# A list scheduler that books the SBUF port of VectorE and GpSimd, with instruction times from a trace

## The chip, the cores and the metric

The program runs on one core of one Trainium2 chip. The metric is device time in microseconds; the time before is the median of 3 runs, 1514.28 us (1511.14 to 1516.61).

## What is computed

A decoder trunk of two layers over one sequence of 512 tokens with 1024 channels, all in float32. Each layer scales and shifts its input by a projection of a condition vector (adaLN), multiplies by one input matrix, and mixes tokens in three ways: a gated recurrence (HGRN2, 256 columns), sparse attention with compressed, selected and windowed keys (512 columns), and a gated MLP over chunks (256 columns). The three are joined by an output matrix, and a squared-ReLU MLP follows. Cut to what matters here:

```python
for l in range(DEPTH):                                   # 2
    sh1, sc1, g1, sh2, sc2, g2 = split(silu(c) @ w_ada[l] + b_ada[l])
    proj = (x * (1 + sc1) + sh1) @ w_in[l]               # 1024 -> 2840
    mix = concat([hgrn2(...), nsa(...), gmlp(...)]) @ w_o[l]
    x = layer_norm(DN_ALPHA * x + (1 + g1) * mix, ln1_w[l], ln1_b[l])
    h = x * (1 + sc2) + sh2
    y = square(relu(h @ w_ff1[l])) @ w_ff2[l]            # 1024 -> 4096 -> 1024
    x = layer_norm(DN_ALPHA * x + (1 + g2) * y, ln2_w[l], ln2_b[l])
```

## The kernel before, in words

**Arithmetic.** A float32 product is made of three float32r products: every operand is split into a high part (a rounding copy, CAST or ACTIVATE) and a low part (a subtraction), and TensorE does high x high, high x low and low x high (`mm3`). Weights are split as they arrive (`wunit`: tiles `whi` and `wlo` of 128x512 or 128x256). The layer's input is transposed on TensorE and scaled, shifted and split into eight pairs `hT` (`make_hT`, two halves of 256 tokens, eight tiles each: an affine copy out of PSUM, a cast for the high part, a subtraction for the low part).

**Stages, once per layer.** Scaled input `hT`; the projections hq, hf and nq; the gated recurrence (tiles `hx` and `hbd`, seven levels); the projections of keys and values and the compressed keys; eight attention units with the remaining projections as filler between them; the state of the recurrence; the output projection (`w_o`) with the first LayerNorm; `make_hT` again, inside `ff`; the MLP in four groups; the second LayerNorm. `affine_rows` (line 1623 before) writes the normalised rows times weight plus bias to the residual stream in DRAM: 16 products and 16 sums of 128x512 tiles `xs`, all on GpSimd, in the stretch in which `make_hT` runs. The adaLN projections (`ada_accs`) are products on VectorE, ScalarE or GpSimd spread over the other stages.

**What sets the order.** The code calls no engine. It writes down instructions with virtual tiles (`Plan.op`), and `Plan.schedule` (line 332 before) places all of them in a model of time: five engines, a price for each instruction (`Plan.cost`), a latency between engines, and slots of SBUF and PSUM. At each step it takes, over all engines, the instruction that can start first; on one engine it goes through the ready ones by priority, which is their place in the program plus a shift. `Plan.emit` then writes them in that order, and each engine works through its queue in that order, whatever the model thought. Some instructions have several engines to choose from: `vg` (VectorE, or GpSimd), `gv` (the other way about), `copy` (ScalarE, or VectorE), `split` (the subtraction on VectorE, or GpSimd where allowed), `scale_rows` (GpSimd, VectorE, ScalarE). The second choice opens once the instruction has been ready for 500 ns:

```python
st = max(slot_time(o, t), bank_time(o, e))
if r[2] and t < o.ready + ALT_WAIT:
    fut = min(fut, max(st, o.ready + ALT_WAIT))
    continue
if st <= t:
    ...
    cand = (t, e, o, r[2])
    break
```

So the prices decide both the order on each queue and which engine does what. In the kernel before, VectorE and GpSimd are priced as if each had SBUF to itself.

All instructions are issued at one line (563 before, 605 after), so the profile is read by tiles and shapes. Tiles of the shared SBUF class are all called `t` in the profile before; the program's names (`hT`, `xs`, `hx`, ...) are told in the text.

Of the kernel before, what the change touches and what calls it, by code (L numbers as in the profile page):

```python
# [36 lines left out]
# ---------------------------------------------------------------- planning  # L37
# Instructions are first written down with virtual tiles, then placed in time by a
# list scheduler with a rough cost of each instruction, and emitted in that order.
# [117 lines left out]
class Op:  # L157
    __slots__ = ("ahead", "alts", "prio", "seq", "reads", "writes", "succ", "nd", "ready", "vts", "newv", "eng", "end",
# [6 lines left out]
NFILL = 1  # L165
STEPS = (1, 1, 2, 2, 2)
# [22 lines left out]
class Plan:  # L189
# [17 lines left out]
    def limit(self, name, n):  # L207
        """at most n tiles of this name live at once"""
        self.add_class("#" + name, n, 0, None)
        self.lims[name] = "#" + name  # L210
# [6 lines left out]
    # ---- cost in ns  # L217
    def cost(self, eng, method, a, k):
# [4 lines left out]
        if eng == "PE":  # L223
            if method == "transpose":
                return (a[1].p1 - a[1].p0) / 1.2 + 2.5
            n = max(int(a[2].idx.size), 32)
            if a[2].dt == F32:
                return max(2 * n / 2.4, a[1].idx.size / 1.2) + 2 * n / 2.4 + 2.5
            return n / 2.4 + 2.5
# [27 lines left out]
        return 100.0  # L257

    def op(self, alts, also=()):
# [56 lines left out]
        o.nd = len(deps)  # L316
        o.succ = []
# [13 lines left out]
    # ---- placement in time  # L331
    def schedule(self):
# [7 lines left out]
               "SP": dict(PE=100.0, V=0.0, A=0.0, G=0.0, SP=0.0)}  # L340
        table = None
# [32 lines left out]
        def slot_time(o, t):  # L374
            """earliest time at which the new tiles of o can have slots; INF: not known yet"""
# [29 lines left out]

        for o in self.ops:
            if o.nd == 0:
                push(o)
# [6 lines left out]
        while n_left:  # L415
            best = None
            for e in T:
# [14 lines left out]
                for r in sorted(ready[e])[:200]:  # L432
# [3 lines left out]
                    st = max(slot_time(o, t), bank_time(o, e))  # L436
# [14 lines left out]
                if cand is None:  # L451
                    for r in pend[e]:
# [5 lines left out]
                        fut = min(fut, max(r[0] + (ALT_WAIT if r[2] else 0), slot_time(o, r[0]), bank_time(o, e)))  # L458
# [13 lines left out]
            start = t  # L472
            if e == "PE":
                load = 0.0
                if alt[1] == "matmul":
                    load = alt[2][1].idx.size / (2.4 if alt[2][1].dt == BF else 1.2)
# [30 lines left out]
            if e == "SP":  # L507
# [4 lines left out]
                dma_free = tr + nbytes / 350.0  # L512
                end = dma_free + 950
                T[e] = start + 460
            else:
                end = start + c
                T[e] = end
            o.done = True
# [25 lines left out]
    def place(self, vt):  # L544
        pool, width = self.classes[vt.cls]["pool"], self.classes[vt.cls]["width"]
        n = int(np.prod(vt.shape[1:]))
        t = pool.tile([128, width], vt.dt, name="%s_%d" % (vt.cls, vt.slot), tag="%s%d" % (vt.cls, vt.slot))
# [19 lines left out]
def trunk(ctx: ExitStack, tc: tile.TileContext, I, out, depth=L):  # L567
# [44 lines left out]
    # ------------------------------------------------------------ constants  # L612
# [12 lines left out]
    # ---- condition vector and the bias of its projection, as columns  # L625
# [21 lines left out]
    # additive masks: causal block [q, k]; compressed blocks per q tile [q, 32]  # L647
# [17 lines left out]
    # level masks of the gated recurrence: [s, t], t in the right half and s in the left half of a block  # L665
# [20 lines left out]
    # rope tables  # L686
# [33 lines left out]
    # vectors that are needed as columns: rows of 128 through the tensor engine  # L720
# [14 lines left out]
    # lower bounds  # L735
# [15 lines left out]
    # ------------------------------------------------------------ helpers  # L751
# [13 lines left out]
    def vg(method, *a):  # L765
        """a product, sum or difference of tiles in SBUF, on either engine"""
# [16 lines left out]
    def wunit(w, off, rowlen, ncols=512, nk=2, held=""):  # L783
        """two k tiles of `ncols` columns of a [*, rowlen] matrix, as high and low parts"""
# [16 lines left out]
    def k_steps(n, steps):  # L801
        """(first k, number of k) of each step over n k tiles: two at a time, or as given"""
# [5 lines left out]
    def tok_steps(xT, w, off, rowlen, ncols, kt, evac, steps=None):  # L808
        """out[tokens, cols] for four token tiles: xT k tiles (hi, lo) stationary, weights moving; a step per two k"""
# [17 lines left out]
    def col_steps(xT, w, off, rowlen, kt, evac, nc_=4, steps=None):  # L827
        """out^T[cols, tokens] for nc_ tiles of 128 columns: weights stationary, xT moving; a step per two k"""
# [945 lines left out]
    xd = x  # L1774
# [65 lines left out]
```

## Time and profile before

| what | value |
|---|---|
| runs, median of 3 (lowest to highest) | 1514.28 us (1511.14 to 1516.61) |
| profiled execution: span from first to last instruction | 1509.3 us |
| median of the runs less that span (launch and end around it, and the difference between executions) | 5.0 us |
| mean granted TensorE clock | 0.971 of full speed |
| TensorE, VectorE, ScalarE, GpSimd busy | 1376.6, 1170.3, 554.9, 462.4 us |

The profiled execution has no time of its own beside its span; sums below are made on the span and carried over to the median of the runs. PE is TensorE, PEld its weight load, DVE VectorE, ACT ScalarE, POOL GpSimd. An instruction counts as busy from when the engine takes it, so time that it waits for something that has no semaphore is inside its duration.

### The profile page before, as it was taken

To read this page: it belongs to the slowest core of one execution; us is meant where nothing else is said; L and a number is where in the kernel's file an instruction comes from. 1 tells how busy PE (TensorE), PEld (TensorE's weight loads), DVE (VectorE), ACT (ScalarE), POOL (GpSimd) and SP (SyncE) were. 2 spreads that over 40 slices of the span, in tenths; PEclk is the share of its full clock that TensorE was granted. 3 is DMA by queue.
4 is the path that set the end of the run, shared out by engine and by line. 5 is a ranking of instruction groups with operands and counts; after the bars stand their busy time and mean duration, and the time that the engine had idled before them with its cause. 6 is when DMAs were issued, how large, how long until landed. Compare 5 with 4: busy or idle time off the path is not lost.

```text
span 1509.3 us, 21620 instructions
## 1 busy us (share of the span) xinstructions
PE 1376.6 (91%) x7459; PEld 1151.8 (76%) x7459; DVE 1170.3 (78%) x2477; ACT 554.9 (37%) x1465; POOL 462.4 (31%) x601
## 2 busy tenths in 40 slices
PE   6867888999879999999998789999896999999996
PEld 4756777777768887888887769888785888888885
DVE  9999979999978557486789995999996663444658
ACT  6541567783203313122314344877421311101121
POOL 6676577453420001010036642223424000000003
PEclk9888999999989999999999899999999999999998
DMA  9521454225466325275414115111454331233331
GB/s 314 183 72 51 119 179 136 71 83 180 152 221 211 132 88 181 97 255 175 147 42 136 35 49 148 30 57 52 147 173 153 126 103 55 94 99 98 111 112 56
DMA packets 119845, 185.69 MB, mean 123 GB/s; under 512 B 9796, under 2 KB 47160, under 8 KB 119736
## 3 DMA queue, kind: packets, MB, share of 16 engines
q1 hardware_dynamic: 119736, 184.31, 38.1%
q8 instruction: 59, 0.97, 0.3%
q14 instruction: 50, 0.41, 0.1%
HBM read 175.89 MB, written 8.39 MB: 122 GB/s over the span
## 4 chain that ended last, share of the span: by engine, by line
PE 64%; DVE 25%; issue 4%; ACT 4%; POOL 2%; DMA 2%; SPq 0%; POOLq 0%; DVEq 0%; ACTq 0%
PE ps L563 64%; DVE t L563 21%; ACT t L563 3%; DVE amax L563 1%; POOL t L563 1%; DMA t<-in_w_ada_dram 1%; DMA raw<-in_w_ada_dram 1%; POOL lnmv L563 1%; DVE acoef L563 1%; DMA t<-in_ln_w_dram 0%; DVE hst L563 0%; POOL hms L563 0%; DVE lt L563 0%; DVE adat L563 0%; POOL gmv L563 0%
## 5 line engine op out<-in xcount | busy, mean ns | idle before, releaser
L563 PE MATMUL ps<-t,t 128*128 128x512 f32 (+5 forms) x6096 | 1261.7, 363 | 72.3 <-DVE t L563 67.2
L563 PEld LDWEIGHTS ps<-t,t 128*128 128x128 f32 x6096 | 1016.5, 193 | 251.8 <-DVE t L563 40.7
L563 ACT ACTIVATE t<-ps 128x512 f32<-128x512 f32 (+11 forms) x462 | 179.0, 413 | 539.9 <-PE ps L563 528.0
L563 POOL TENSOR_TENSOR t<-t,t 128x512 f32<-128x512 f32 (+5 forms) x244 | 241.4, 1004 | 255.4 <-ACT t L563 133.1
L563 DVE TENSOR_TENSOR t<-raw,t 128x512 fp32r<-128x512 f32 (+2 forms) x376 | 248.2, 678 | 13.7 <-ACT t L563 7.2
L563 POOL TENSOR_TENSOR t<-raw,t 128x512 fp32r<-128x512 f32 (+2 forms) x56 | 65.6, 1176 | 535.7 <-ACT t L563 368.5
L563 DVE TENSOR_TENSOR t<-t,t 128x512 fp32r<-128x512 f32 (+6 forms) x270 | 182.2, 694 | 5.9 <-ACT t L563 0.8
L563 DVE TENSOR_TENSOR t<-t 128x512 f32<-128x512 f32 (+1 forms) x94 | 60.1, 653 | 151.7 <-ACT t L563 151.6
L563 ACT ACTIVATE t<-raw 128x512 fp32r<-128x512 f32 (+2 forms) x241 | 128.4, 568 | 129.3 <-DMA raw<-in_w_ff_dram 107.5
L563 PE MATMUL ps<-ident,t 128*128 128x128 f32 (+1 forms) x635 | 110.7, 282 | 36.8 <-DVE t L563 20.4
L563 ACT ACTIVATE t<-t 128x512 fp32r<-128x512 f32 (+5 forms) x202 | 98.1, 510 | 112.0 <-DVE t L563 95.8
L563 PEld LDWEIGHTS ps<-ident,t 128*128 128x128 f32 (+1 forms) x635 | 75.9, 144 | 57.6 <-issue 18.3
L563 DVE TENSOR_TENSOR t<-ps,t 128x512 fp32r<-128x512 f32 (+5 forms) x237 | 109.3, 482 | 9.1 <-ACT t L563 3.9
L563 DVE SCALAR_TENSOR_TENSOR t<-raw,silc,t 128x512 f32<-128x512 f32 x98 | 74.6, 773 | 10.7 <-DMA raw<-in_w_ada_dram 9.4
L563 DVE CAST t<-raw 128x512 fp32r<-128x512 f32 (+2 forms) x191 | 81.4, 430 | 0.2
L563 ACT ACTIVATE t<-ps,amax 128x128 f32<-128x128 f32 (+3 forms) x128 | 67.3, 534 | 20.2 <-DVE amax L563 18.4
L563 DVE TENSOR_TENSOR t<-t,ps 128x512 f32<-128x512 f32 (+1 forms) x48 | 31.1, 650 | 53.7 <-PE ps L563 53.5
L563 DVE TENSOR_REDUCE amax<-ps 128x1 f32<-128x32 f32 (+4 forms) x192 | 65.5, 380 | 4.0 <-PE ps L563 3.1
L563 POOL TENSOR_SCALAR t<-t,acoef 128x384 f32<-128x384 f32 (+3 forms) x55 | 32.2, 599 | 67.6 <-DVE acoef L563 51.7
L563 ACT ACTIVATE t<-ps,adasb 128x256 f32<-128x256 f32 x48 | 23.4, 571 | 72.4 <-PE ps L563 72.4
L563 POOL TENSOR_SCALAR t<-raw,silc 128x512 f32<-128x512 f32 x48 | 37.3, 782 | 27.4 <-PE ps L563 9.9
L563 POOL TENSOR_SCALAR lnmv<-lnmv 128x1 f32<-128x1 f32 x16 | 5.6, 348 | 113.8 <-DVE lnmv L563 113.8
(141 smaller groups left out, 878.5 us busy)
## 6 DMA issues: line engine op xcount, KB each, us to landing
raw<-in_w_ff_dram SPq DMA_DIRECT2D x128, 512.0 KB, 4.5
raw<-in_w_ada_dram SPq DMA_DIRECT2D x80, 512.0 KB, 4.6
raw<-in_w_in_dram SPq DMA_DIRECT2D x49, 256.0 KB, 2.9
t<-in_w_ada_dram SPq DMA_DIRECT2D x32, 256.0 KB, 6.1
raw<-in_w_o_dram SPq DMA_DIRECT2D x16, 512.0 KB, 4.0
raw<-in_w_in_dram SPq DMA_DIRECT2D x15, 512.0 KB, 3.6
xd<-t SPq DMA_DIRECT2D x24, 256.0 KB, 2.2
t<-xd SPq DMA_DIRECT2D x24, 256.0 KB, 4.9
```

Of the source, the lines that this page charges most:

```text
L563: getattr(self.handles[e], method)(*a, **k)
```

## The change

Five things change in `Plan`. All touch only the model of time; no instruction's arithmetic is changed, and the counts stay at 7301 TensorE instructions and 470 DMAs.

1. A port is booked. `shares` says which instructions use it: all of GpSimd's but `memset` and `iota`; on VectorE those with two inputs in SBUF, and `tensor_copy` and `tensor_scalar` from SBUF to SBUF. VectorE may start one only from 69 ns before GpSimd's last one ends, GpSimd from 147 ns before VectorE's.
2. TensorE's prices: a float32r product of n columns costs n / 2.246 + 4 ns (n / 2.4 + 2.5 before), a float32 product two passes of at least 111 ns each, and a weight load 4 ns more.
3. A VectorE instruction that needs news of more than one engine starts 62 ns later for each further one.
4. A DMA moves 310 bytes per ns (350 before).
5. Tiles are named by the program's names in the profile.

```diff
+OPEN_V, OPEN_G = 69.0, 147.0
+WAIT = 62.0
...
             if a[2].dt == F32:
-                return max(2 * n / 2.4, a[1].idx.size / 1.2) + 2 * n / 2.4 + 2.5
-            return n / 2.4 + 2.5
+                return 2 * max(2 * n / 2.4 + 2.5, 111.0)
+            if a[2].dt == BF:
+                return n / 2.4 + 2.5
+            return n / 2.246 + 4.0
...
+    def shares(self, eng, method, a, k):
+
+        if eng == "G":
+            return method not in ("memset", "iota")
+        if eng != "V" or method == "memset":
+            return False
+        out = k.get("out", a[0] if a else None)
+        ins = [x for x in list(a[1:]) + [x for n, x in k.items() if n != "out"] if isinstance(x, VA)]
+        ins = [v for v in ins if v.vt.cls not in self.psum and (v.idx.size > 1 or out.idx.size == 1)]
+        if method in ("tensor_copy", "tensor_scalar"):
+            return bool(ins) and out.vt.cls not in self.psum
+        return len(ins) > 1
...
+        def port_time(o, ai, e):
+            if e not in port or not o.port[ai]:
+                return 0.0
+            return port["G"] - OPEN_V if e == "V" else port["V"] - OPEN_G
...
-                    st = max(slot_time(o, t), bank_time(o, e))
+                    st = max(slot_time(o, t), bank_time(o, e), port_time(o, r[2], e))
...
+            if e == "V" and news > 1:
+                start += WAIT * (news - 1)
...
-                    load = alt[2][1].idx.size / (2.4 if alt[2][1].dt == BF else 1.2)
+                    load = 4 + alt[2][1].idx.size / (2.4 if alt[2][1].dt == BF else 1.2)
...
-                dma_free = tr + nbytes / 350.0
+                dma_free = tr + nbytes / 310.0
...
+                if e in port and o.port[ai]:
+                    port[e] = end
```

**What moves.** Over the whole program VectorE goes from 2477 to 2250 instructions, GpSimd from 601 to 753, ScalarE from 1261 to 1336 (table loads and accumulator reads left out). By the part of the program that an instruction belongs to:

| part | VectorE | GpSimd |
|---|---|---|
| layer 0 up to the attention (and the setup) | 438 to 402 | 187 to 218 |
| layer 0 attention | 363 to 324 | 117 to 146 |
| layer 0 `make_hT` in `ff` | 40 to 31 | 20 to 25 |
| layer 0 MLP | 423 to 392 | 38 to 48 |
| layer 1 up to the attention | 299 to 252 | 78 to 112 |
| layer 1 attention | 366 to 338 | 77 to 94 |
| layer 1 MLP | 369 to 351 | 19 to 34 |

First place: VectorE in layer 1, second half of the tokens of `make_hT` inside `ff`, before. The rows follow the last normalised row tile; a CAST makes a high part, a TENSOR_TENSOR of 128x256 a low part.

```order
L563 TENSOR_SCALAR t_32_12619<-t_32_12619,lnmv_12648 128x512
L563 CAST t_54_12509<-t_40_12700 128x256
L563 SCALAR_TENSOR_TENSOR t_44_12569<-ps_12690,t_44_12569 128x512
L563 TENSOR_TENSOR t_59_12519<-t_40_12700,t_54_12509 128x256
L563 CAST t_68_12514<-t_63_12707 128x256
L563 CAST t_12_12528<-t_36_12714 128x256
L563 TENSOR_TENSOR t_43_12522<-t_63_12707,t_68_12514 128x256
L563 TENSOR_TENSOR t_34_12536<-t_36_12714,t_12_12528 128x256
L563 CAST t_65_12545<-t_60_12731 128x256
L563 CAST t_22_12547<-t_62_12741 128x256
L563 TENSOR_TENSOR t_58_12541<-t_57_12722,t_9_12533 128x256
```

Five more such rows and one weight subtraction follow, before VectorE goes on with the weights. The same place after, VectorE:

```order
L605 TENSOR_SCALAR r_12619<-r_12619,lnmv_12636 128x512
L605 TENSOR_SCALAR hf_66_12709<-ps_12693,adasb_7551 128x256
L605 CAST hT_12532<-hf_0_12705 128x256
L605 SCALAR_TENSOR_TENSOR grow_12560<-ps_12707,grow_12560 128x512
L605 TENSOR_SCALAR hf_30_12734<-ps_12716,adasb_7551 128x256
L605 TENSOR_TENSOR hT_12527<-hf_12_12697,hT_12516 128x256
L605 TENSOR_TENSOR hT_12545<-hf_66_12709,hT_12535 128x256
L605 TENSOR_TENSOR hT_12562<-hf_30_12734,hT_12554 128x256
L605 TENSOR_TENSOR wlo_12775<-wraw_12215,whi_12761 128x512
```

and GpSimd, where before only the `xs` of `affine_rows` stood:

```order
L605 TENSOR_TENSOR xs_12700<-r_12315,lnw_12568 128x512
L605 TENSOR_TENSOR xs_12721<-r_12320,lnw_12568 128x512
L605 TENSOR_TENSOR hT_12521<-hf_60_12688,hT_12511 128x256
L605 TENSOR_TENSOR hT_12540<-hf_0_12705,hT_12532 128x256
L605 TENSOR_TENSOR hT_12557<-hf_75_12727,hT_12549 128x256
L605 TENSOR_TENSOR hT_12573<-hf_59_12738,hT_12564 128x256
L605 TENSOR_TENSOR hT_12581<-hf_77_12743,hT_12571 128x256
L605 TENSOR_TENSOR xs_12700<-xs_12700,lnb_12578 128x512
```

Of the sixteen casts and subtractions of this half VectorE did fourteen; it keeps one cast and three subtractions; five subtractions stand on GpSimd ahead of the rest of `xs`, and seven casts on ScalarE. VectorE does two affine copies out of PSUM in their stead.

Second place: the start of the gated recurrence in layer 0 (tiles `hx`, `hbd`). GpSimd after, where one `hx` or `hbd` follows the other:

```order
L605 TENSOR_TENSOR hx_1261<-hgk_973,hgq_938 128x512
L605 TENSOR_TENSOR hx_1272<-hgk_985,hgq_944 128x512
L605 TENSOR_TENSOR hx_1287<-hb_1277 128x8x32
L605 TENSOR_TENSOR hx_1290<-hb_1277 128x16x16
L605 TENSOR_TENSOR hx_1294<-hb_1277 128x32x8
L605 TENSOR_TENSOR hx_1290<-hb_1277 128x16x16
L605 TENSOR_TENSOR hbd_817<-hx_1287,hgq_938 64x4x64 x2
L605 TENSOR_TENSOR hx_1294<-hb_1277 128x32x8
```

and VectorE after, in the same stretch of the plan, in which the rotary products of the query projections (out of PSUM, tiles `acc`) now stand between the levels instead of behind them:

```order
L605 TENSOR_TENSOR hx_1355<-hb_1277 128x256
L605 TENSOR_TENSOR hx_1352<-hb_1309 128x128x2
L605 TENSOR_TENSOR hx_1357<-hb_1309 128x256
L605 TENSOR_SCALAR sin_81<-sin_81 128x4x32
L605 TENSOR_TENSOR ropet_1369<-acc_355,sin_81 128x4x32
L605 TENSOR_TENSOR ropet_1371<-acc_355,sin_81 128x4x32
L605 TENSOR_TENSOR ropet_1375<-acc_398,sin_81 128x4x32
```

There are 16 such products of 128x4x32 and 8 of 128x256 in a row. The query projection of the second half, which came after the recurrence before, is moved ahead of most of its levels.

## Rows read from the trace of the kernel before

**Rows 1.** The page, part 1: span, busy time and share of two engines

```profile
span 1509.3 us, 21620 instructions
PE 1376.6 (91%) x7459; PEld 1151.8 (76%) x7459; DVE 1170.3 (78%) x2477; ACT 554.9 (37%) x1465; POOL 462.4 (31%) x601
```

**Rows 2.** By stretch, us busy: PE, PEld, DVE, ACT, POOL, granted clock, DMA share, GB/s

```profile
0.00:198.00 198.00, 150.61 (x903) 129.79 (x903) 178.42 (x445) 90.04 (x226) 124.58 (x203) 0.91 0.51 158
198.00:339.00 141.00, 128.30 (x894) 107.41 (x894) 135.72 (x358) 108.12 (x368) 88.39 (x109) 0.99 0.33 100
...
397.00:426.00 29.00, 15.86 (x119) 14.42 (x118) 26.32 (x30) 5.27 (x12) 25.08 (x22) 0.91 0.26 82
426.00:778.00 352.00, 351.09 (x1557) 286.27 (x1558) 241.66 (x413) 83.77 (x149) 21.74 (x17) 0.99 0.49 163
778.00:936.00 158.00, 133.19 (x910) 120.85 (x909) 133.15 (x299) 60.45 (x158) 87.61 (x108) 0.95 0.30 90
936.00:1061.00 125.00, 122.95 (x884) 104.31 (x883) 114.22 (x335) 97.94 (x342) 37.77 (x64) 1.00 0.18 57
...
1122.00:1151.00 29.00, 17.23 (x124) 15.02 (x122) 26.99 (x30) 7.40 (x15) 23.84 (x21) 0.95 0.33 117
1151.00:1490.00 339.00, 338.96 (x1481) 276.30 (x1482) 187.41 (x324) 59.15 (x103) 8.77 (x7) 0.99 0.31 97
1490.00:1509.40 19.40, 7.07 (x54) 6.61 (x53) 14.26 (x25) 2.78 (x5) 9.66 (x11) 0.74 0.30 109
```

**Rows 3.** What PE waited for, five stretches in order: us in total, times, longest

```profile
PE ps L563 <- DVE t L563: 29.0, 16, 8.6
...
PE ps L563 <- DVE t L563: 9.7, 14, 2.2
...
PE ps L563 <- DVE t L563: 13.0, 4, 8.5
...
PE ps L563 <- DVE t L563: 21.7, 15, 5.6
...
PE ps L563 <- DVE t L563: 11.8, 4, 6.6
```

**Rows 4.** Timeline of DVE from 395 us, first half of make_hT: start, us, count

```profile
395.04 0.49 DVE L563 CAST t<-t 128x256 fp32r<-128x256 f32 x2
395.44 0.76 DVE L563 TENSOR_TENSOR t<-t,t 128x256 fp32r<-128x256 f32 x2
```

**Rows 5.** DVE by shape, 409 to 426 us, second half: count, busy us, mean ns

```profile
L563 DVE TENSOR_TENSOR t<-t,t 128x256 fp32r<-128x256 f32 x8 | 9.4, 1202 | 0.0
L563 DVE CAST t<-t 128x256 fp32r<-128x256 f32 x7 | 8.2, 1209 | 0.0
```

**Rows 6.** Timeline of POOL from 405 us: the products and sums of affine_rows

```profile
405.47 19.37 POOL L563 TENSOR_TENSOR t<-t,t 128x512 f32<-128x512 f32 x14
```

**Rows 7.** DVE by shape, 198 to 339 us: source in PSUM and in SBUF

```profile
L563 DVE TENSOR_TENSOR t<-ps,t 128x512 fp32r<-128x512 f32 x40 | 25.9, 681 | 0.6 <-PE ps L563 0.2 <-ACT t L563 0.2
...
L563 DVE TENSOR_TENSOR t<-raw,t 128x512 fp32r<-128x512 f32 x4 | 4.9, 1216 | 0.0
```

**Rows 8.** DVE by shape, 500 to 540 us, inside the MLP

```profile
L563 DVE TENSOR_TENSOR t<-raw,t 128x512 fp32r<-128x512 f32 x14 | 9.0, 685 | 0.1
```

**Rows 9.** DVE and POOL by shape, whole span

```profile
L563 DVE SCALAR_TENSOR_TENSOR t<-t,t 128x256 f32<-128x256 f32 x16 | 6.4, 416 | 0.1
...
L563 DVE TENSOR_TENSOR t<-ps,sin 128x128 f32<-128x128 f32 x32 | 8.8, 286 | 0.3
...
L563 POOL TENSOR_TENSOR t<-t,t 128x256 f32<-128x256 f32 x49 | 40.6, 833 | 44.7 <-DVE t L563 33.2 <-ACT t L563 10.5
```

**Rows 10.** DVE by shape, 778 to 936 us, where make_hT of layer 1 runs

```profile
L563 DVE TENSOR_TENSOR t<-t,t 128x256 fp32r<-128x256 f32 x10 | 9.1, 942 | 0.0
L563 DVE CAST t<-t 128x256 fp32r<-128x256 f32 x8 | 9.0, 1154 | 0.0
```

**Rows 11.** The chain that ended last, piece from 1135 us: start, us, engine, count

```profile
1135.39 15.61 DVE t L563 x13
```

More of the change, by code (lines that the diff above doesn't have):

```diff
@@ L157 @@
 class Op:
-    __slots__ = ("ahead", "alts", "prio", "seq", "reads", "writes", "succ", "nd", "ready", "vts", "newv", "eng", "end",
+    __slots__ = ("ahead", "alts", "port", "deps", "eng_no", "prio", "seq", "reads", "writes", "succ", "nd", "ready", "vts", "newv", "eng", "end",
                  "tabs", "banks", "done")
@@ L316, in op @@
         o.nd = len(deps)
+        o.deps = list(deps)
         o.succ = []
@@ L340, in schedule @@
                "SP": dict(PE=100.0, V=0.0, A=0.0, G=0.0, SP=0.0)}
+        count = {e: 0 for e in T}
+        seen = {e: {} for e in T}
         table = None
@@ L404, in bank_time @@
             return max([vt.bank_end for vt in o.banks if vt.bank_eng != e], default=0.0)
+        def port_time(o, ai, e):
+            if e not in port or not o.port[ai]:
+                return 0.0
+            return port["G"] - OPEN_V if e == "V" else port["V"] - OPEN_G
         for o in self.ops:
+            o.port = [self.shares(*alt) for alt in o.alts]
             if o.nd == 0:
@@ L457, in schedule @@
                             continue
-                        fut = min(fut, max(r[0] + (ALT_WAIT if r[2] else 0), slot_time(o, r[0]), bank_time(o, e)))
+                        fut = min(fut, max(r[0] + (ALT_WAIT if r[2] else 0), slot_time(o, r[0]), bank_time(o, e),
+                                           port_time(o, r[2], e)))
                     if fut < INF:
@@ L472, in schedule @@
             start = t
+            o.eng_no = (e, count[e])
+            count[e] += 1
+            news = 0
+            last = {}
+            for d in o.deps:
+                x, i = d.eng_no
+                last[x] = max(last.get(x, -1), i)
+            for x, i in last.items():
+                if i > seen[e].get(x, -1):
+                    seen[e][x] = i
+                    news += 1
+            if e == "V" and news > 1:
+                start += WAIT * (news - 1)
             if e == "PE":
@@ L546, in place @@
         n = int(np.prod(vt.shape[1:]))
-        t = pool.tile([128, width], vt.dt, name="%s_%d" % (vt.cls, vt.slot), tag="%s%d" % (vt.cls, vt.slot))
+        t = pool.tile([128, width], vt.dt, name="%s_%d" % (vt.name, vt.slot), tag="%s%d" % (vt.cls, vt.slot))
         ap = t[:vt.shape[0], :n]
```

## Prediction
> **What bounds the kernel now.** The page comes first: TensorE is busy 1376.6 of 1509.3 us [rows 1], so 132.7 us at most are to be had without making its work shorter. Then the stretches between the changes of stage [rows 2]. The two MLPs, 426 to 778 us and 1151 to 1490 us, are TensorE's: it is busy 351.1 of 352 us and 339.0 of 339, and nothing that the other engines do better there can show. The attention of layer 1 is nearly so (123.0 of 125). Time without TensorE work lies elsewhere: 47.4 us in the opening (198 less 150.6), 12.7 in the attention of layer 0, 13.1 at the first LayerNorm (397 to 426), 24.8 at the start of layer 1 (778 to 936), 11.8 at its LayerNorm (1122 to 1151) and 12.3 in the tail. These six make 122 of the 132.7.
>
> Next, the waits. In the first five of these stretches TensorE waits for VectorE 29.0, 9.7, 13.0, 21.7 and 11.8 us [rows 3]: VectorE is late, not the loads. VectorE is busy 178 of 198, 136 of 141, 26 of 29, 133 of 158 and 27 of 29 us there [rows 2].
>
> Then why VectorE is slow. In the first half of `make_hT` with GpSimd quiet, two casts of 128x256 take 0.49 us and two subtractions 0.76 [rows 4], so 245 and 380 ns each. In the second half the same shapes take 1209 and 1202 ns [rows 5], while GpSimd runs 14 products and sums of 128x512 in 19.37 us without a gap, 1384 ns each [rows 6]. Each VectorE instruction there lasts about as long as one of GpSimd's. It is not so for all: in the attention a subtraction with its source in PSUM takes 681 ns and one with both inputs in SBUF 1216 [rows 7], against 685 ns for that shape in the MLP, where GpSimd has little to do [rows 8]. So GpSimd holds VectorE up when both want SBUF, and only then. That is what the new model books.
>
> **The change, part by part.** The work is the same; what moves is who does it, and when. Instructions dropped by VectorE and taken by GpSimd stand in the table of the change; means are stretch busy time over count [rows 2].
>
> *Opening, to 198 us.* VectorE drops 36 at 401 ns (178.42/445): -14.4 us. GpSimd takes 31 at 614 ns (124.58/203): +19.0. If every one of them waits its turn at the port, the net is +4.6; if GpSimd's are all beside other work, -14.4. The order shows other work: 16 rotary products out of PSUM at 286 ns and 8 twice as wide, taken at 416 ns [rows 9], now stand beside GpSimd's run of `hx`, 7.9 us that need no port. I take 4.6 - 7.9 = **-3**.
>
> *Attention of layer 0.* VectorE drops 39 at 379 ns, -14.8; GpSimd takes 29 at 811 ns, +23.5; net +8.7 if all queue. The gain is capped by TensorE's 12.7 us of idle time. Much of VectorE's work here reads PSUM and can run beside GpSimd, which is what the model now looks for. I take about half the cap, **-6**.
>
> *First LayerNorm.* The port's queue for the second half: before, 15 casts and subtractions in 17.6 us [rows 5]. After, the order has four subtractions (4 x 0.38) and one weight subtraction (0.685) [rows 4, 8] on VectorE, three `xs` (3 x 1.38) [rows 6] and four subtractions at 833 ns [rows 9] on GpSimd: 9.7 us. That is 7.9 less. But in the new order three more `xs` stand on GpSimd ahead of the reciprocal root that the last row tile waits for: +4.2. I take **-3**; the ends are -7.9 and +4.2.
>
> *Start of layer 1.* The same `make_hT` pattern: 8 casts and 10 subtractions take 9.0 + 9.1 us [rows 10]. The order moves the 8 casts to ScalarE and 7 subtractions to GpSimd; 3 x 0.38 + 7 x 0.833 = 7.0 us, 11 less. In the whole stretch VectorE drops 47 at 445 ns (-20.9) and GpSimd takes 34 at 811 ns (+27.6), a net +6.7 where they queue. 6.7 - 11 gives -4; the port can't give more than TensorE's wait, 21.7. I take **-5**.
>
> *LayerNorm of layer 1.* Here the chain is 15.61 us of VectorE [rows 11], and nothing is put ahead of the last tile. After: one cast, three subtractions (1.4 us), two `xs` (2.8), five subtractions on GpSimd (4.2): 8.3 us. **-7**, with a cap of 11.8. ScalarE's seven casts cost nothing: it is busy 7.4 of 29 us. If it were late the casts would be late, and at most this gain goes.
>
> *Tail.* Two sums of the last row tile go from VectorE to GpSimd, the last of them on the path: 0.83 instead of 0.42 us [rows 9] and one more hand-over. **+1**; the ends are 0 and +2.
>
> *The rest.* MLPs 0: VectorE drops 31 and 18 instructions, GpSimd takes 10 and 15, all beside TensorE, which is covered by 100% busy time; without that cover GpSimd's 25 would cost some 25 us at about 1 us. The new prices of products, loads and DMA only move order, on SP too: three adaLN loads pass weight loads in the opening, with DMA engines busy 0.51 of the time. 0.
>
> Sum: -3 - 6 - 3 - 5 - 7 + 1 = -23. On the span 1509.3 that is 1486; the median of the runs lies 5.0 above, so **1491 us**.
>
> A rule against this change: the Trainium skill, GPSIMD Engine Reference, § 8 Key points, says that for elementwise work VectorE is structurally about twice as fast. The trace agrees: 833 against 416 ns for 128x256 [rows 9]. By that rule alone every instruction given to GpSimd holds the port twice as long, and opening, attention and layer 1's start would lose as in the first rival below.
>
> **The rivals.** *GpSimd's longer hold decides (slower).* The planner gives GpSimd 152 more instructions, because VectorE now looks later. In the opening, the attention and the start of layer 1 these are 94, and if all of them queue, the nets are +4.6, +8.7 and +6.7. With the LayerNorms at -3 and -7 and the tail at +1 that makes +11: **1525**. It wins from the point at which GpSimd's 94 (70 us) hold VectorE for more than the 50 us that VectorE drops there. For it: the opening keeps GpSimd 125 of 198 us busy already. Against it: TensorE waits on VectorE, not on GpSimd.
>
> *The plan doesn't hold (no change).* The queues are fixed ahead and the chip lets whoever comes first into SBUF. A plan that is off by some hundred ns puts VectorE behind GpSimd again; the stalls come back elsewhere and eat what the LayerNorms give: **1514**. For it: the model has many prices that are off by more than this.
>
> *Most stalls go (faster still).* If each of the five stretches comes half-way from my term to its end (-14.4, -12.7, -7.9, -21.7, -11.8; tail 0: -68), the sum is (-23 - 68)/2 = -46: **1468**.
>
> **How the numbers follow.** Forecast 0.55, with a range of its own of 1479 to 1504; slower rival 0.20; no change 0.13; faster still 0.12. A measurement here tells 0.3% (4.5 us) from no change. Faster is 0.55 + 0.12 = 0.67, same 0.13, slower 0.20. The range runs from 1466, just below the third rival, to 1528, just above the first; outside are the outer parts of both, some 0.15.
>
> **What would show it.** In the changed profile: busy VectorE down by more than the dropped instructions account for; casts and subtractions of 128x256 below 700 ns in the second half at both LayerNorms; TensorE's wait there below 7 us; MLP stretches unchanged within 1 us. Wrong, if GpSimd's busy time in the opening passes 145 us and VectorE's means there do not fall; if the last row tile's normalisation at the first LayerNorm comes over 4 us later than before; or if TensorE's idle total stays near 133 us.

## The result, and the profile after

The changed kernel takes **1475.37 us** (median of 4 runs, 1473.22 to 1476.26) against 1514.41 of the kernel before on the same chip (1511.14 to 1516.61): a ratio of 0.9741, 95% interval 0.9727 to 0.9756. It is faster by 39 us. The forecast was 1491, its range 1466 to 1528. The profiled spans differ by 35.7 us (1509.3 and 1473.6): the median now lies 1.8 us above the span, and lay 5.0 above it before.

The page of the changed kernel, part 1, answers to [rows 1]:

```profile
span 1473.6 us, 21673 instructions
PE 1369.8 (93%) x7459; PEld 1150.7 (78%) x7459; DVE 1104.8 (75%) x2250; ACT 588.1 (40%) x1543; POOL 589.2 (40%) x753
```

TensorE's idle time is 103.8 us (1473.6 less 1369.8), 132.7 before. Where it went is read stage by stage. A stage ends here when its last instruction ends, taken from the timeline at the same place of the program in both kernels: the last compressed value, the last low part of the attention's output, the eighth `ffa` tile of the MLP (its first group of products), and the last normalised row tile after MLP 0 or the last sum of half a row tile in MLP 1; the tail runs to the span's end. So the first LayerNorm's stage runs from the attention's end through the output projection, the normalisation and `make_hT` to the MLP's first eight tiles. The filler products have no fixed stage, so a stage can also become shorter because work left it. The last columns keep the two apart: TensorE's idle time in the stage, and its matmuls (one that crosses a border counts on both sides).

| stage, us | before | after | difference | predicted | idle before, after | matmuls before, after |
|---|---|---|---|---|---|---|
| opening of layer 0 | 203.5 | 216.4 | +12.9 | -3 | 48.6, 60.9 | 942, 969 |
| attention of layer 0 | 137.1 | 120.2 | -16.9 | -6 | 11.6, 7.1 | 861, 766 |
| first LayerNorm and `make_hT` | 122.4 | 124.1 | +1.7 | -3 | 16.2, 8.3 | 553, 623 |
| MLP 0 | 328.6 | 327.7 | -0.9 | 0 | 2.9, 1.9 | 1471, 1471 |
| start of layer 1 | 150.8 | 137.8 | -13.0 | -5 | 23.2, 11.6 | 876, 885 |
| attention of layer 1 | 117.9 | 111.3 | -6.6 | 0 | 1.7, 2.1 | 821, 769 |
| LayerNorm and `make_hT` of layer 1 | 126.8 | 116.0 | -10.8 | -7 | 16.3, 1.8 | 583, 626 |
| MLP 1 | 292.7 | 292.8 | +0.1 | 0 | 0.0, 0.0 | 1266, 1266 |
| tail | 29.5 | 27.3 | -2.2 | +1 | 12.2, 10.0 | 98, 99 |

The sum is -35.7, the difference of the spans: 28.9 us less idle time and 6.8 us less busy time. Layer 1 before its MLP gives 30.4 of it (395.5 to 365.1), 25.7 of that in idle time. Layer 0 before its MLP gives 2.3 (463.0 to 460.7) and nothing in idle time (76.4 and 76.3): the opening loses what the attention and the LayerNorm gain. Both attentions became shorter mainly because matmuls moved out of them, into the stages beside them: 95 matmuls and 12.4 us of busy time in layer 0, 52 and 7.0 us in layer 1.

**Layer 1's LayerNorm is where the change works as meant.** VectorE and then GpSimd in its second half, timelines of the changed kernel (start, us, engine):

```profile
1113.36 1.22 DVE L605 CAST hT<-hf 128x256 fp32r<-128x256 f32 x1 [0.31 <-ACT hf L605]
1114.50 0.68 DVE L605 SCALAR_TENSOR_TENSOR grow<-ps,grow 128x512 f32<-128x512 f32 x1
1115.10 0.53 DVE L605 TENSOR_SCALAR hf<-ps,adasb 128x256 f32<-128x256 f32 x1
1115.55 2.34 DVE L605 TENSOR_TENSOR hT<-hf,hT 128x256 fp32r<-128x256 f32 x3
```

```profile
1114.39 4.10 POOL L605 TENSOR_TENSOR hT<-hf,hT 128x256 fp32r<-128x256 f32 x5
1118.44 1.74 POOL L605 TENSOR_TENSOR xs<-xs,lnb 128x512 f32<-128x512 f32 x1
```

The half is done in 5.1 us (1113.36 to 1118.49), where the chain before had 15.61 us of VectorE [rows 11]. One VectorE instruction is not as fast as forecast: the cast takes 1.22 us and a subtraction 780 ns. VectorE has 4 of them here instead of 14. The chain of waits passes through this place on other engines now:

```profile
1103.58 8.01 PE acc L605 x68
1111.59 0.23 PE ps L605 x2
...
1111.85 1.49 ACT hf L605 x3
...
1115.62 2.26 DVE hT L605 x3
1117.89 1.16 DVE wlo L605
...
1119.08 2.95 PE acc L605 x15
```

TensorE is busy 13.65 of the 14 us here, 17.23 of 29 before [rows 2]. The windows (columns as in [rows 2]):

```profile
409.00:427.00 18.00, 13.74 (x82) 12.00 (x81) 14.73 (x18) 7.81 (x18) 17.76 (x16) 0.81 0.44 146
...
788.00:926.00 138.00, 126.19 (x886) 115.27 (x884) 111.34 (x266) 69.52 (x206) 103.28 (x133) 0.95 0.34 101
926.00:1037.00 111.00, 108.87 (x766) 92.23 (x766) 99.80 (x273) 92.01 (x312) 38.74 (x70) 1.00 0.15 43
1105.00:1119.00 14.00, 13.65 (x105) 12.38 (x103) 13.14 (x20) 7.70 (x18) 13.25 (x15) 1.00 0.06 20
```

**In the first LayerNorm TensorE stands still for 7.9 us less, although the stage is 1.7 us longer.** It holds 70 more matmuls. The second half of `make_hT` takes 7.3 us (419.05 to 426.34; 17.6 before, [rows 5]), but the last row tile is normalised at 418.6 us, not 408.4, although the attention ended 4 us earlier. Two things make it late. The larger one lies ahead of GpSimd: the mean and variance of that tile are ready at 410.8 us, 403.4 before. Before, VectorE made the pairs of the first half between the row tiles (393.8 to 398.3 us); now TensorE transposes that half only at 400.5 us, behind all products of `w_o`, and VectorE makes its pairs and normalises the third tile (402.1 to 408.1 us) before it turns to the last. The smaller one is on GpSimd: the reciprocal root (`lnmv`, two small instructions) stands behind and between products and sums of `xs` and is ready 4.8 us after the variance, 2.1 before. The place before, VectorE and GpSimd:

```profile
403.15 0.21 DVE L563 BATCH_NORM_AGGREGATE lnmv<-lnst 128x2 f32<-128x12 f32 x1
403.45 0.19 POOL L563 TENSOR_SCALAR lnmv<-lnmv 128x1 f32<-128x1 f32 x1 [1.68 <-DVE lnmv L563]
403.72 1.29 POOL L563 TENSOR_TENSOR t<-t,t 128x512 f32<-128x512 f32 x1
404.96 0.54 POOL L563 TENSOR_TENSOR lnmv<-lnmv,mhalf 128x1 f32<-128x1 f32 x1
...
405.54 2.89 DVE L563 TENSOR_SCALAR t<-t,lnmv 128x512 f32<-128x512 f32 x2 [2.18 <-POOL lnmv L563]
```

and after, VectorE's statistics and then GpSimd:

```profile
410.59 0.21 DVE L605 BATCH_NORM_AGGREGATE lnmv<-lnst 128x2 f32<-128x12 f32 x1
```

```profile
409.24 1.74 POOL L605 TENSOR_TENSOR xs<-r,lnw 128x512 f32<-128x512 f32 x1
411.06 1.61 POOL L605 TENSOR_TENSOR xs<-xs,lnb 128x512 f32<-128x512 f32 x1
412.75 0.52 POOL L605 TENSOR_SCALAR lnmv<-lnmv 128x1 f32<-128x1 f32 x1
413.34 1.78 POOL L605 TENSOR_TENSOR xs<-r,lnw 128x512 f32<-128x512 f32 x1
415.09 0.54 POOL L605 TENSOR_TENSOR lnmv<-lnmv,mhalf 128x1 f32<-128x1 f32 x1
```

VectorE's normalisation, released at 415.6, then takes 2.89 us for two instructions beside the next `xs`, as long as before.

**In the opening TensorE stands still once, for 34.7 us.** What TensorE waited for up to 216 us, and the row of its timeline:

```profile
PE ps L605 <- DVE qrope L605: 34.7, 1, 34.7
PE ps L605 <- POOL adacc L605: 6.8, 1, 6.8
```

```profile
129.22 0.99 PE L605 MATMUL ps<-heads,hx 128*128 128x2 f32 x4 [34.70 <-DVE qrope L605]
```

The rotary products `qrope` read the query projections out of PSUM. They need the tables, and the cosine table is ready at 128.3 us, 68.7 before. Until then TensorE's next matmul, which belongs to the recurrence, waits. Two other lists planned with the port, told of below, stand nearly as long in the opening: 32.2 us (the old engines, ordered by the new model) and 32.8 (the port alone). In the second TensorE waits for ScalarE's split of a weight, which stands directly behind the cosine in ScalarE's queue (126.3 us).

### The profile page after: what moved, and what is told of

Its sections match the earlier page's. It is cut to its first block, busy times and chain, and to the rows that moved or that the text cites. A ratio compares the mean times of both kernels' runs of the same rounds, so it can differ in the third digit from the quotient of the medians.

```text
span 1473.6 us, 21673 instructions
## 1 busy us (share of the span) xinstructions
PE 1369.8 (93%) x7459; PEld 1150.7 (78%) x7459; DVE 1104.8 (75%) x2250; ACT 588.1 (40%) x1543; POOL 589.2 (40%) x753
## 4 chain that ended last, share of the span: by engine, by line
PE 68%; DVE 13%; POOL 9%; ACT 5%; issue 4%; DMA 1%; SPq 0%; POOLq 0%; ACTq 0%; DVEq 0%
PE acc L605 55%; PE aps L605 8%; PE ps L605 5%; DVE wlo L605 2%; DVE adacc L605 1%; POOL hx L605 1%; POOL xs L605 1%; POOL adacc L605 1%; ACT P L605 1%; POOL hbd L605 1%; DVE rt L605 1%; POOL wloh L605 1%; DVE hatt L605 1%; DVE lnst L605 1%; DVE hT L605 1%
## 5 line engine op out<-in xcount | busy, mean ns | idle before, releaser
L605 PE MATMUL acc<-hT,whi 128*128 128x512 f32 (+1 forms) x1296 | 413.6, 375 | 8.3 <-ACT hT L605 4.0
L605 PE MATMUL acc<-whi,aT 128*128 128x512 f32 x896 | 325.1, 394 | 0.0
L605 PEld LDWEIGHTS acc<-hT,whi 128*128 128x128 f32 x1296 | 236.1, 191 | 54.6 <-ACT hT L605 4.7
L605 DVE TENSOR_TENSOR wlo<-wraw,whi 128x512 fp32r<-128x512 f32 (+2 forms) x313 | 233.6, 766 | 18.4 <-ACT whi L605 12.3
L605 PE MATMUL acc<-hT,wlo 128*128 128x512 f32 (+1 forms) x648 | 237.1, 373 | 0.6 <-DVE wlo L605 0.6
L605 PE MATMUL acc<-whi,hT 128*128 128x256 f32 (+2 forms) x1024 | 229.5, 310 | 1.4 <-DVE grow L605 1.0
L605 PEld LDWEIGHTS acc<-whi,aT 128*128 128x128 f32 x896 | 168.1, 188 | 39.6
L605 PEld LDWEIGHTS acc<-whi,hT 128*128 128x128 f32 x1024 | 170.6, 193 | 8.4 <-DVE grow L605 1.2
L605 PE MATMUL acc<-wlo,aT 128*128 128x512 f32 x448 | 176.7, 394 | 0.0
L605 PE MATMUL acc<-wlo,hT 128*128 128x256 f32 (+2 forms) x512 | 158.0, 309 | 0.0
L605 PEld LDWEIGHTS acc<-hT,wlo 128*128 128x128 f32 x648 | 122.4, 190 | 25.4 <-DVE wlo L605 2.8
L605 PEld LDWEIGHTS acc<-wlo,aT 128*128 128x128 f32 x448 | 84.1, 188 | 19.5
```

Source lines behind the costliest of these rows:

```text
L605: getattr(self.handles[e], method)(*a, **k)
```

## The experiments

All ratios are to the kernel before on the same chip, 4 runs each. "Front" is layer 0 up to its MLP (463.0 us before, 460.7 after), "middle" is layer 1 up to its MLP (395.5 and 365.1), both from the timelines of the profiled runs.

**The parts of the change.** The port alone, with the old prices and no extra wait:

```diff
-WAIT = 62.0
+WAIT = 0.0
...
-                dma_free = tr + nbytes / 310.0
+                dma_free = tr + nbytes / 350.0
```

and the old matmul and weight-load prices likewise.

> The change with the booked port alone: prices of TensorE, loads, DMA and the 62 ns wait as before. Theory 'port' (the gain comes from booking the port): 1470 to 1485 us, most of the 39 us. Rival 'prices' (the gain comes from truer TensorE and DMA times): 1505 to 1520. If both give half each: about 1495.

1479.54 us (1478.02 to 1485.69), 0.9781 [0.976, 0.9802]; front 455.3, middle 376.9.

The new prices without the port:

```diff
-            o.port = [self.shares(*alt) for alt in o.alts]
+            o.port = [False for alt in o.alts]
```

> The change without the port (nothing uses it), with all new prices and the 62 ns wait. Theory 'port': 1505 to 1520 us, no gain beyond what another order gives by chance. Rival 'prices': 1475 to 1490.

1533.26 us, 1.0121 [1.0099, 1.0143]; front 473.1, middle 409.8. At its first LayerNorm VectorE's pairs take as long as before [rows 5]; VectorE by shape, 420 to 480 us:

```profile
L605 DVE TENSOR_TENSOR hT<-hf,hT 128x256 fp32r<-128x256 f32 x8 | 9.4, 1204 | 0.0
L605 DVE CAST hT<-hf 128x256 fp32r<-128x256 f32 x6 | 6.8, 1180 | 0.0
```

The whole change without its 62 ns wait (`WAIT = 0.0`):

> The change without the 62 ns that a VectorE instruction pays for each further engine it hears from. It is a detail of the prices: 1470 to 1482 us if details don't matter; above 1485 if VectorE's true pace matters as much as the port.

1473.22 us, 0.9729 [0.9713, 0.9746]; front 457.4, middle 369.6. So the gain is the port's: prices alone lose 19 us, the port alone gives 34.5, and the wait gives no gain (1473.2 without it, 1475.4 with it). The 4 us between the port alone and the whole change are less than one list differs from the next, as shown below.

**Which engine, or in which order.** Every instruction with several engines to choose from is held to the engine that the other kernel's plan gave it; the order is then planned by the model of the kernel that is edited: the engines of after under the model of before, and the other way about. `PIN` holds one letter for each such instruction.

```diff
+    free = [o for o in plan.ops if len(o.alts) > 1]
+    for o, e in zip(free, PIN):
+        o.alts = [alt for alt in o.alts if alt[0] == e]
     order = plan.schedule()
```

> Each instruction runs on the engine that the change gave it (GpSimd 749, VectorE 2250), but the order is made by the model of before, which books no port. Theory 'order' (the gain is that VectorE does PSUM work while GpSimd holds the port): 1500 to 1530 us, since the longer holds of GpSimd stay and nothing is put beside them. Rival 'engines' (the gain is the work taken off VectorE): 1475 to 1490.

1534.11 us, 1.0133 [1.0118, 1.0148]; front 509.9, middle 373.3.

> Each instruction runs on the engine that it had before (GpSimd 597, VectorE 2477), ordered by the model of the change. Theory 'order': 1475 to 1490 us. Rival 'engines': 1505 to 1520. If order and engines are only worth something together, both crossed kernels stay above 1500.

1529.01 us, 1.01 [1.0081, 1.012]; front 486.3, middle 396.9. Both stay above 1500 us: in total each half of the change loses. But in the middle, the engines of the changed kernel give 22 us (395.5 to 373.3) under a model that knows no port, and the order alone gives none (396.9). The other lists say the same of the middle. Where the engines were chosen with the port it takes 362.8 to 376.9 us (seven lists, those below among them), where they were chosen without it 390.7 to 409.8 (five). In front both crossed kernels lose: the second stands 32.2 us for the rotary tables, and in the first, where engines chosen for one order stand late in another, TensorE waits 34.9 us for GpSimd up to 370 us.

```profile
PE ps L581 <- POOL t L581: 34.9, 9, 17.3
```

VectorE's busy time, in which its waits for the port are counted, goes by the engines too: with the new ones it is 1097.8 us under the old model and 1104.8 under the new, with the old ones 1170.3 and 1166.4. So booking the port does not make VectorE wait less in all. It makes the planner choose other engines, ScalarE and GpSimd, for some of VectorE's work. How the gain divides between these two was not tried.

**More GpSimd without the port.** The kernel before, with `ALT_WAIT = 0.0` (500.0), so that second choices open at once:

> The kernel before with the model's wait before an instruction goes to its second-choice engine cut from 500 ns to 0, and no port: GpSimd then gets more of the instructions that can run on either engine, and VectorE fewer. Theory (more work on GpSimd costs VectorE the port, unless the list knows of it): slower than before, 1520 to 1545, with GpSimd busy above the 594 us or so of before. Rival (the engines alone are the gain, and the port is only a way to get them): as fast as the changed kernel, 1470 to 1490. Rival (scatter): anywhere from 1490 to 1535.

1532.89 us, 1.0121 [1.0105, 1.0136]; front 472.7, middle 404.5. GpSimd gets 713 instructions (601 before, 753 after; busy 621.8 us; before it was 462.4, not the 594 of the expectation), and 19 us are lost. But the edit opens second choices on VectorE as well: ScalarE loses 73 instructions (1261 to 1188) where the change gave it 75, and VectorE drops only 39. So the run shows that more GpSimd is no gain by itself, and not what the changed kernel's engines would give without the port; that is the first crossed kernel. GpSimd at layer 1's LayerNorm, timeline of this run, to be set beside the 4.10 us for five above:

```profile
1162.58 8.57 POOL L563 TENSOR_TENSOR t<-t,t 128x256 fp32r<-128x256 f32 x6 [1.27 <-ACT t L563]
```

Six subtractions take 1428 ns each; VectorE's casts and subtractions stand beside them. The Trainium skill, Perfetto Trace Analysis, section Optimizing Scalar/DVE Operations, warns that moving work between VectorE and GpSimd may not help, since they share a port. This run goes the same way (19 us slower with 112 more GpSimd instructions), and the changed kernel, with 152 more, does not.

**How far a list scatters.** The kernel before with one price changed (`nbytes / 310.0`):

> The kernel before with one price changed, the divisor of the model's DMA bytes (350 to 310, as in the change), and no port. It moves the list without telling the scheduler anything of the port, so it shows how far a list scatters by itself. Theory (it is the knowledge of the port that gives the 39 us): within 20 us of the kernel before, 1500 to 1535, as prices alone gave 1533, and the products and sums of the first LayerNorm still beside GpSimd, its stretch 118 to 128 us. Rival (a list moved in any way lands anywhere between 1470 and 1535, and the changed kernel is one lucky draw): 1490 or less is possible, one time in three.

1506.35 us, 0.9948 [0.9934, 0.9963]; front 466.9, middle 390.7. The total is where the theory had it, but the stages moved more than expected: attention of layer 0 +14.8 us (8.8 of it idle time), the first LayerNorm's stage -7.4, to 115.0, outside the 118 to 128 expected. So a stage of layer 0 says little by itself. The totals say more: four lists whose engines were chosen without the port (1506, 1514, 1533, 1533) and four chosen with it (1473, 1475, 1480, and 1495 of the run below) do not overlap, and their means are 41 us apart. The lists of each four are near relatives, though, and the crossed kernels (1534 and 1529) show that the engines do not bring the total without the order made for them.

**What GpSimd's products cost by the port.** In both kernels the 32 products and sums of `affine_rows` become `memset`s, which need no input. The affine of the LayerNorms is left out of the output.

```diff
-                E.tensor_mul(t, r[j][half], wt)
-                E.tensor_add(t, t, bt)
+                E.memset(t, 1.0)
+                E.memset(t, 0.5)
```

> The kernel before, with the 32 products and sums of the row affine step after each of three LayerNorms replaced by as many memsets of the same tiles on GpSimd, so that GpSimd is busy (about half as long) without using the port; the affine step is left out of the result. Theory 'port': casts and subtractions of 128x256 in the second half at both first LayerNorms fall from 1200 ns to 250 and 390, and each of the two stretches gives back 7 to 11 us, the end of the first MLP 0 to 5: 1490 to 1500 us. Rival (VectorE is slow there for another reason, such as late inputs): the means stay over 1000 ns and the time within 5 us of before.

1482.14 us, 0.9781 [0.976, 0.9803]: -32 us, more than expected. First LayerNorm's stage -14.6 us, start of layer 1 and its LayerNorm -8.4 each. VectorE by shape at the first LayerNorm, 400 to 420 us:

```profile
L563 DVE TENSOR_TENSOR t<-t,t 128x256 fp32r<-128x256 f32 x8 | 3.0, 417 | 0.0
L563 DVE CAST t<-t 128x256 fp32r<-128x256 f32 x7 | 2.9, 451 | 0.5 <-ACT t L563 0.5
```

These are the shapes that took 1202 and 1209 ns [rows 5]. The plan has 2477 VectorE instructions as before, the opening and the attention, where no `xs` stands, take 203.9 and 137.1 us (203.5 and 137.1 before), and `xs` goes to the residual stream, not to these pairs. So this is what GpSimd's products and sums cost by standing beside VectorE. The memsets are not as neutral as expected. They are shorter (0.6 us each) and over at 408.6 us, with more than half of the pairs still to come. The first three casts, beside them, take 630 to 655 ns and the subtractions there 370 to 420; behind them a cast takes 245 again. At layer 1's LayerNorm it is the same (casts 630 and 655 ns beside the memsets, 240 to 245 behind). So a `memset` on GpSimd, which the planner's `shares` leaves out, goes with a slower cast here, and hardly with a slower subtraction.

> The same replacement in the changed kernel; the affine step is left out of the result. What is left of the port's cost at the LayerNorms in the changed kernel: if the change has already taken it, 1468 to 1476 us; if GpSimd's products still cost at the first LayerNorm (its last row tile comes 10 us later than before), 1460 to 1467.

1467.48 us, 0.9689 [0.9674, 0.9704], 8 us below the changed kernel: first LayerNorm -5.5, start of layer 1 -2.1, layer 1's LayerNorm +0.8. By these two runs the change has taken back 24 of the 32 us. Where the other 8 are is less sure: this list is another one (VectorE has 2290 instructions, 2250 in the changed kernel), and MLP 0 moved by -3.1 as well.

**The stall in the opening.** The changed kernel with the rotary tables written early (their place in the program no longer shifted back by 800):

```diff
+    plan.shift = 0
     inv = static([128, 32], F32, "inv")
...
+    plan.shift = 800
     rows = big((76, 128), name="rows")
```

> The change, with the rotary tables (sin, cos) given the priority of the rest of the opening instead of 800 places behind. In the changed kernel's trace TensorE stands still for 34.7 us from 94 to 129 us: the banks of PSUM with the query projections are held until the tables are there. Theory 'late tables' : the wait falls below 15 us and the run takes 1455 to 1466 us. Rival (the port's queue in the opening is the bound, and the tables only stand in its way): 1472 to 1480, the wait comes back at the recurrence.

1495.3 us, 0.9871 [0.9849, 0.9893]. Neither theory had this. The 34.7 us wait is gone (the longest in the opening is 6.0) and the opening is 9.6 us shorter, but attention of layer 0 grows from 120.2 to 153.1 us. TensorE's waits in this run, 216 to 360 us:

```profile
PE ps L605 <- POOL adacc L605: 15.9, 2, 12.9
PE aps L605 <- POOL P L605: 5.5, 7, 3.1
```

The attention's next matmuls stand behind the transposition of an adaLN vector, whose sum GpSimd has not finished. Those vectors are layer 0's own, for its first residual sum and its MLP's input; their 48 products and 42 sums of 128x512 are GpSimd's in both kernels.

**The same, with ScalarE making those 48 products.**

```diff
-        r = layer(l, yn, xd, sb, rest(0, nxt, "G") if l == 0 else iter(()), nxt)
+        r = layer(l, yn, xd, sb, rest(0, nxt, "A") if l == 0 else iter(()), nxt)
```

> The changed kernel, with the products of layer 0's adaLN vectors for layer 1 on ScalarE instead of GpSimd. They are 32 or so instructions of GpSimd that hold the port. Theory (the change has left 8 us to be had from the port, most of it at the first LayerNorm, as its twin without the affine's products showed): 1465 to 1475, the gain in the first LayerNorm and in attention of layer 0, ScalarE busier by 20 to 40 us. Rival (ScalarE's exponentials end last in attention, so work on ScalarE is worse than on GpSimd): 1480 to 1500, attention of layer 0 longer by 5 us or more. Rival (the list moves, and that decides): anywhere from 1470 to 1495, the stages before attention moved as well.

1460.84 us (1457.09 to 1465.84), 0.965 [0.9621, 0.9679]; front 446.4, middle 365.1. The products are 48, not 32, and for layer 0, not for layer 1 as the expectation has it. The total is below the theory's range by 4 us; ScalarE is 22.6 us busier. Against the changed kernel the opening gives 9.4 us and the first LayerNorm 11.1; attention takes 6.2 us more, as the first rival had it, which fell in the total. Some 45 matmuls moved back from the LayerNorm's stage to the attention, so in idle time these two are -3.6 and +1.5. That the first LayerNorm gains is not explained by the products, which are over by then, so a part of this is the list. The root of the last row tile now stands ahead of the second `xs` there.

> As the run before it (the products of layer 0's adaLN vectors on ScalarE), and with the rotary tables early as well. With the tables early alone the opening was 10 us shorter and attention of layer 0 33 us longer, since a transposition of a vector stood in TensorE's queue and waited for GpSimd's sum. Theory (that wait is for GpSimd, which has too much to do there): with the products on ScalarE the wait for GpSimd's sum is under 4 us, the opening keeps 5 to 10 us, and the total is 1458 to 1470. Rival (the place of the transposition in the list is what is wrong, whichever engine makes the sum): the wait is there for ScalarE's or VectorE's work, 8 us or more, and the total 1480 to 1500.

**1451.95 us** (1448.17 to 1454.09), 0.9586 [0.9568, 0.9604], the fastest version: 62 us below the kernel before and 23 below the changed one; front 435.0, middle 362.8. Early tables cost 20 us in the changed kernel and give 9 here. Attention takes 123.3 us, and the wait for GpSimd's sum is gone; TensorE's longest waits, 216 to 360 us:

```profile
PE aps L605 <- DVE PT L605: 3.9, 3, 1.7
PE ps L605 <- DVE hst L605: 1.1, 3, 0.5
```

The total is 6 us below the theory's range, the rival's 1480 to 1500 is out, and the opening is 19.5 us shorter than the changed kernel's (196.9), twice what was expected. Whether ScalarE's products would help the kernel before as well was not tried.

## Why the prediction came out as it did

**What held.** The bound was read rightly: the MLPs moved by 0.9 and 0.1 us, and the idle time that went lies outside them but for 1.0 us. The hold of the port was there to be taken back, as the pairs in the run with `memset`s show. The forecast for layer 1's LayerNorm came by its mechanism (casts to ScalarE, subtractions to GpSimd ahead of `xs`): 8.3 us forecast for the half and 5.1 measured; -7 forecast for the stage and -10.8 measured, -14.5 in idle time, of which 3.2 us are a wait for the recurrence's state (`hst`, 4.5 to 1.3) that no term had. TensorE's wait at the LayerNorms fell below 7 us, to 4.3 (409 to 427) and 0.3 us (1105 to 1119).

**The total: right side, by errors of both signs.** -23 was forecast and -35.7 measured on the spans; the 5.0 us for the median, 1.8 now, add 3.2 to the distance. 1475 lies 4 us outside the forecast's own range of 1479 to 1504; it is inside the stated one because that reached down to the third rival. The opening came out 16 us worse than its term and the others together 29 us better, so the total is nearer than its parts, and that is luck. The terms and their caps were idle time of TensorE, and that is what they are held against below.

**Opening, -3, measured +12.9 (idle +12.3).** The step that failed is the sign. The sum was made of VectorE's and GpSimd's net; what decided was a late table and a full TensorE queue, which no term had. The rotary products were read as cover for GpSimd's `hx`; that the sine stands behind the recurrence's levels was in the order rows too, and was not read as a wait of TensorE. Without that wait (tables early) the opening is 206.8 us, still 3.3 above before, so the -3 is not seen there either. The sign given for being wrong is half there: GpSimd is busy 155.4 us up to 216, but 142.4 up to 203, and VectorE's mean fell only from 401 to 395 ns (171.71/435).

**Attention of layer 0, -6, measured -16.9 (idle -4.5).** In idle time the term was near. The rest of the 16.9 us, more than the cap of 12.7 allows, is the 12.4 us of TensorE's work that moved out. Opening and attention together went from 340.6 to 336.6, and by the runs above this scatters from 320 to 371 us from list to list. Half-caps at single stages of layer 0 claimed more than such a list allows.

**First LayerNorm, -3, measured +1.7 (idle -7.9).** Both ends of the term occurred: the half is 10.3 us shorter (7.9 forecast), and the last row tile is later by the mechanism named (`xs` ahead of the root), 2.7 us where +4.2 was put. The tile is 10.2 us later in all, over the 4 us that were given as a sign of being wrong; most of that comes from the late transposition, behind the matmuls that moved into the stage, which the sum did not have. TensorE was busy with that work and waited only 1.8 us for the tile. So the -3 between the two ends was too small, and the sign did not show what it was meant to show.

**Start of layer 1, -5, measured -13.0 (idle -11.5).** The mechanism was right: the `hT` tiles alone are 9.4 us earlier against the MLP's end. The +6.7 of queueing set against it did not come: the largest of TensorE's waits for VectorE there adds up to 5.1 us, 21.7 before [rows 3].

**Attention of layer 1, 0, measured -6.6 (idle +0.4).** It was put at nothing since TensorE was busy 123.0 of 125 us, and in idle time nothing came. The stage is shorter because 52 matmuls left it.

**Tail, +1, measured -2.2.** Small, and the wrong sign: the two sums on GpSimd take 1.85 us together and do not make the tail longer.

**A sign that was wrong.** VectorE's busy time was to fall by more than its dropped instructions account for. It fell by 65.5 us, and 227 instructions at the old mean of 472 ns are 107. Those that are left got longer where both inputs are in SBUF. Weight subtractions before and after, and subtractions with one input in PSUM after (681 ns before, [rows 7]), whole span:

```profile
L563 DVE TENSOR_TENSOR t<-raw,t 128x512 fp32r<-128x512 f32 x284 | 201.0, 726 | 7.0 <-ACT t L563 2.2
```

```profile
L605 DVE TENSOR_TENSOR wlo<-wraw,whi 128x512 fp32r<-128x512 f32 x248 | 195.2, 806 | 10.8 <-ACT whi L605 5.7 <-issue 0.7
...
L605 DVE TENSOR_TENSOR PT<-aps,PT 128x512 fp32r<-128x512 f32 x80 | 51.0, 683 | 5.2 <-PE aps L605 2.1 <-ACT PT L605 2.0 <-PE acc L605 0.4
```

The pairs at the LayerNorms stayed above 700 ns as well (813 and 803 at the first).

**The rivals.** GpSimd's longer hold did not decide. It is there, as the weight subtractions show, but TensorE hardly waited for it: the start of layer 1, with 34 more on GpSimd, gained 13.0 where the rival had +6.7. The prediction took a rule from the Trainium skill, GPSIMD Engine Reference, § 8 Key points, that VectorE is about twice as fast for elementwise work. The 833 against 416 ns [rows 9] stand, but the loss that was drawn from them did not come. That the plan does not hold fell too: with the port, lists made with other prices and waits gave 1473 to 1480. "Most stalls go" (1468) came nearest in size, in layer 1 alone.

## What to carry to other kernels

Where two engines share a resource, put it into the planner before refining prices: finer prices alone lost 19 us here, the port alone gave 34.5, and the gain came with the engines that the planner then chose, in the order made for them. Judge a change of a list scheduler by several lists with and without it and by the sum of neighbouring stages, since one price can move a single stage by 15 us while the total moves by 8. Read a stage by the idle time of the engine that bounds it, not by its length: here 95 matmuls moved from one stage to its neighbours and looked like a gain of 12 us. When a list is better in all, look for the one long wait at the head of an in-order queue; taking away two such waits (a late table, an adaLN sum) went with 23 us more here, while the first alone cost 20.

## What was not expected of the hardware

After TensorE's 34.7 us of standing still the granted clock is low, and stays low for a while when work is back. The windows of the changed kernel, columns as in [rows 2]:

```profile
60.00:94.00 34.00, 33.83 (x202) 29.57 (x202) 28.54 (x49) 15.76 (x29) 31.32 (x29) 1.00 0.53 166
94.00:129.00 35.00, 0.52 (x2) 0.00 (x0) 33.36 (x66) 19.82 (x30) 26.03 (x30) 0.54 0.00 0
129.00:140.00 11.00, 10.79 (x58) 10.43 (x58) 8.69 (x24) 3.03 (x8) 10.22 (x13) 0.59 0.39 100
140.00:150.00 10.00, 7.95 (x48) 6.37 (x48) 9.62 (x23) 5.34 (x14) 8.65 (x12) 1.00 0.01 3
```

From 129 to 140 us it is 0.59, near the lower level of 1.2 GHz, with TensorE busy 10.79 of 11 us, and 1.00 from 140. Transpositions of 128x128 (`ident` by `qrope`) take 404 ns in that stretch, and 272 ns (`ident` by `krope`) from 150 us; the products `hbd` by `hx` take 362 and 279 ns. So such a wait costs more than itself: by these means some 2.5 to 3.5 of the 10.8 us of work (an estimate).
